# Loading the first group of x in two pieces, both ahead of the opening barrier, in a fused LoRA kernel

## The chip, the cores and the metric

One core of one Trainium2 chip. The time is device microseconds (us) of an execution, the median of several runs; of the 33 executions of the kernel before that were timed beside the experiments, 31 lie within 0.3% of the median of their call (123.17 to 123.88 us in all). The profile of an execution covers a *span*, from the first instruction to the last, which here is about 2 us less than the time (121.3 us against 123.23 us in the profiled run of the kernel before). All runs compared below are listed as fast unless the text says otherwise.

## The reference

```python
# x: (16, 512, 768), A: (768, 16), B: (16, 768), float32; scale = 0.5
def reference(x, A, B, scale):
    lora = np.matmul(np.matmul(x, A), B)
    return (x + scale * lora).astype(np.float32)
```

x is read once and the output is written once, 25.2 MB each. The arithmetic is small.

## The kernel before

The 8192 rows of x are cut into 8 groups of 1024. A group is one tile of 128 partitions with 8 rows of 768 floats each, so a partition's part of a group is 24 KB and lies in one piece in memory. Six such tiles exist. ScalarE casts a group to fp16, VectorE transposes it in blocks, TensorE multiplies by A and B, VectorE adds the product to x in place, and the tile is stored. The engines wait for each other, and for transfers, by semaphores (counters). The sync engine (SP) issues every transfer. Its first load is moved into the program's first block, ahead of the barrier at which the engines meet at the start (ScalarE's first instruction behind it comes at 0.95 us):

```python
def load(g):
    nc.sync.dma_start(out=xs[g % X_BUFS], in_=view(x2, g)).then_inc(loaded[g], 16)

def sync_program():
    ...                                   # (cut: switches symbolic addresses off and on)
    load(0)
    now, first = nc.cur_bb.bb.instructions, nc.main_func.blocks[0].instructions
    at = next(k for k, i in enumerate(first)
              if i.engine == mybir.EngineType.SP and isinstance(i, mybir.InstDrain))
    first.insert(at, now.pop())           # ahead of the barrier
    nc.sync.dma_start(out=a32..., in_=A...).then_inc(a_in, 16)   # 384 pieces of 128 B
    nc.sync.dma_start(out=b32, in_=B).then_inc(b_in, 16)         # 16 pieces of 3 KB
    for g in range(1, X_BUFS):
        load(g)
    for g in range(NG - 1):
        nc.sync.wait_ge(added, 4 * (g + 1) + 2)
        ...                               # store group g; then load groups 6 and 7

def scalar_program():
    cast(0, 0, G // 2)._wait_ge(loaded[0], 16)
    cast(0, G // 2, G // 2)
    cast(1, 0, G)._wait_ge(loaded[1], 16)
    ...                                   # (cut)
```

Of the kernel before, what the change touches and what calls it, by code (L numbers as in the profile page):

```python
# [11 lines left out]
G = 8  # L12

X_BUFS = 6
# [4 lines left out]
def kernel(  # L19
# [14 lines left out]
    nc = tc.nc  # L34
# [5 lines left out]
    x2 = x.flatten_outer_dims()  # L40
# [14 lines left out]
    xs = [x_0] + [const.tile([P, G, D], fp32, name=f"x_{i}") for i in range(1, X_BUFS)]  # L55
# [15 lines left out]
    def semaphore(name):  # L71
        sems.append(nc.alloc_semaphore(name))
        return sems[-1]

    loaded = [semaphore(f"loaded_{g}") for g in range(NG)]
# [14 lines left out]
    def view(ap, g):  # L90
        return ap[ds(g * P * G, P * G), :].rearrange("(p s) d -> p s d", s=G)

    def load(g):
        nc.sync.dma_start(out=xs[g % X_BUFS], in_=view(x2, g)).then_inc(loaded[g], 16)

    def sync_program():
        symbolic, nc._always_lower_symbolic_ap = nc._always_lower_symbolic_ap, False
        load(0)
        nc._always_lower_symbolic_ap = symbolic

        now, first = nc.cur_bb.bb.instructions, nc.main_func.blocks[0].instructions
        at = next(
            k for k, i in enumerate(first)
            if i.engine == mybir.EngineType.SP and isinstance(i, mybir.InstDrain)
        )
        first.insert(at, now.pop())
        nc.sync.dma_start(  # L107
            out=a32.rearrange("i (b r) -> i b r", b=NB),
            in_=A.rearrange("(b i q) r -> i b (q r)", i=Q, q=2),
        ).then_inc(a_in, 16)  # L110
        nc.sync.dma_start(out=b32, in_=B).then_inc(b_in, 16)  # L111
# [4 lines that stand above are left out]
            nc.sync.dma_start(out=view(out2, g), in_=xs[g % X_BUFS]).then_inc(  # L116
                freed[g] if g < len(freed) else stored, 16
            )
            if g == len(freed) - 1:
                for n in range(X_BUFS, NG):  # L120
                    nc.sync.wait_ge(freed[n - X_BUFS], 16)
                    load(n)

        nc.sync.wait_ge(added, 4 * NG + 2)
        nc.sync.sem_clear(range(nums[0], nums[-1] + 1))
# [15 lines left out]
    def cast(g, s0, n):  # L141
        rows = ds(s0, n)
        i = nc.scalar.copy(out=xh[g % 2][:, rows, :], in_=xs[g % X_BUFS][:, rows, :])  # L143
        i.then_inc(ready, 1)
        return i

    def scalar_program():
        cast(0, 0, G // 2)._wait_ge(loaded[0], 16)
        cast(0, G // 2, G // 2)
        cast(1, 0, G)._wait_ge(loaded[1], 16)  # L150
        for g in range(NG):
            for a in range(NQ):
                q = ds(a * Q, Q)
                i = nc.scalar.mul(out=y_diag[q, :, q], in_=y_ps[q, :, :], mul=sc)  # L154
                if a == 0:
                    i._wait_ge(ready, min(g + 3, NG + 1) + g + 1)
            i.then_inc(spread, 1)
            if g + 2 < NG:
                cast(g + 2, 0, G)._wait_ge(loaded[g + 2], 16)
# [86 lines left out]
    with tc.tile_critical(no_gpsimd_drain=True):  # L246
        sync_program()
        pool_program()
        scalar_program()
        vector_program()  # L250
        tensor_program()
# [37 lines left out]
```

## Time and profile before

| | before |
|---|---|
| time, median of 3 | 123.54 us (123.49 to 123.57) |
| span of the profiled run | 121.3 us |
| moved | 50.43 MB |
| first data packet, after the first issue | 1.00 us |
| mean end of the 16 DMA engines' last packets | 119.30 us |
| last engine's last packet | 120.04 us |

The last three rows are read from the DMA records of the trace, one record per packet. A packet here is one contiguous piece, 24 KB of x or of the output (2048 of the 2736 packets; the others are 384 of 128 B, 16 of 3 KB and 288 of 4 B).

The profile's page, before: busy time of the engines, then in 40 equal slices of the span the busy share of the DMA engines in tenths and the rate, then the queue's busy share. In all the profile's lines PE is TensorE and PEld its weight loads, DVE is VectorE, ACT is ScalarE, POOL is GpSimd and SPq the sync engine; L94 is line 94 of kernel.py, and x4 is a count. The page counts 16 DMA engines, and the GB/s are what they moved; what is issued to them and not yet moved is here called the queue.

```profile
PE 52.1 (43%) x323; PEld 30.6 (25%) x323; DVE 84.2 (69%) x48; ACT 55.9 (46%) x42; POOL 4.9 (4%) x9
...
DMA  7999999999999999999999999999999999999991
GB/s 227 421 392 419 397 478 413 397 478 421 397 478 405 413 470 413 413 454 430 413 446 438 413 438 446 413 438 438 421 438 438 413 446 438 413 446 438 413 454 73
...
q1 hardware_dynamic: 2736, 50.43, 97.8%
```

VectorE is the busiest compute engine, at 69%. The DMA engines are busy 97.8% of the span, and every slice but the first and the last is near full.

The stage windows, before (stretch, its length, busy time of each engine with its instructions, granted clock, DMA share, rate):

```profile
core 0: us, PE busy (x) PEld busy (x) DVE busy (x) ACT busy (x) POOL busy (x), PEclk, DMA share, GB/s
...
1.00:2.00 1.00, 0.00 (x0) 0.00 (x0) 0.00 (x0) 1.00 (x1) 0.86 (x3) 1.00 1.56 393
2.00:3.00 1.00, 0.00 (x0) 0.00 (x0) 0.00 (x0) 0.23 (x1) 1.00 (x2) 1.00 0.70 295
3.00:4.00 1.00, 0.00 (x0) 0.00 (x0) 0.00 (x0) 0.00 (x0) 1.00 (x1) 1.00 0.99 418
4.00:8.00 4.00, 0.00 (x0) 0.00 (x0) 0.00 (x0) 0.00 (x0) 1.81 (x2) 1.00 0.97 418
...
9.00:11.00 2.00, 0.00 (x0) 0.00 (x0) 0.21 (x1) 0.59 (x1) 0.00 (x0) 1.00 1.17 391
...
13.00:110.00 97.00, 50.84 (x320) 30.36 (x320) 82.10 (x44) 52.02 (x41) 0.00 (x0) 0.95 1.00 431
```

The windows book a packet whole in the stretch where it starts, so a stretch as short as a packet (0.9 us) can show over 1.00: sixteen 24 KB packets that start between 1 and 2 us make the 393 GB/s of that row, though they land later. Over long stretches this evens out: from 13 to 110 us the share is 1.00 at 431 GB/s.

The timeline, before (start, duration, engine, line, what; in brackets what the engine waited for): the first issues and the first cast, and the last two stores.

```profile
0.00 0.38 SPq L94 DMA_DIRECT2D x<-in_x_dram  x1
...
0.99 0.34 SPq L107 DMA_DIRECT2D a_70<-in_A_dram  x1
...
2.16 0.41 SPq L94 DMA_DIRECT2D x_61<-in_x_dram  x1
...
10.41 5.41 ACT L143 CAST xh_66<-x 128x3072 f16<-128x3072 f32 x2 [8.18 <-DMA x<-in_x_dram]
...
96.11 0.33 SPq L116 DMA_DIRECT2D out_dram<-x  x1
106.12 0.33 SPq L253 DMA_DIRECT2D out_dram<-x_61  x1
```

And pieces of the chain of waits that ended last, before (start, duration, what):

```profile
2.16 15.90 DMA x_61<-in_x_dram
...
18.09 5.32 ACT xh_67 L143
...
23.43 3.38 DVE xt L166
...
98.87 6.75 DVE x_61 L197 x4
```

This chain runs through ScalarE, VectorE and TensorE, and its shares by engine begin with "DVE 44%". Read alone it says that compute sets the end. The DMA records say otherwise. The last store is issued at 106.1 us, while a full group takes 8 packets of 0.912 us on each engine, 7.3 us. Work issued earlier fills the queue until about 112.7 us on the engine that ends last, so the last store is there some 6.6 us before its turn.

### The profile page before, as it was taken

The numbers are of one execution on the slowest core, as the hardware profiler recorded it, in microseconds if no ns is written. First come the engines' busy times: TensorE is split into PE (matmuls) and PEld (weight loads), VectorE is DVE, ScalarE is ACT, GpSimd is POOL, SyncE is SP. The second block draws the span as 40 slices with busy tenths as digits, with TensorE's granted clock in tenths as the row PEclk, the third lists the DMA queues.
The fourth block names the chain that finished last, engine by engine and source line by source line (L and its number), as shares of the span: only waits on it lengthen the run. The fifth ranks groups of instructions, "written<-read, shape, count | busy, mean of one in ns | idle before, by whom it ended". The sixth has DMA issues, their size and how long they took to land.

```text
span 121.3 us, 888 instructions
## 1 busy us (share of the span) xinstructions
PE 52.1 (43%) x323; PEld 30.6 (25%) x323; DVE 84.2 (69%) x48; ACT 55.9 (46%) x42; POOL 4.9 (4%) x9
## 2 busy tenths in 40 slices
PE   0003109576944684294375449437446745000000
PEld 0000006331622362172144227216213522000000
DVE  0004990299959999999999999999999639800000
ACT  4005929989159719917943395992400220000000
POOL 6900000000000000000000000000000000000000
PEclk9999999965699999999999999999999999975555
DMA  7999999999999999999999999999999999999991
GB/s 227 421 392 419 397 478 413 397 478 421 397 478 405 413 470 413 413 454 430 413 446 438 413 438 446 413 438 438 421 438 438 413 446 438 413 446 438 413 454 73
DMA packets 2736, 50.43 MB, mean 416 GB/s; under 512 B 672, under 2 KB 672, under 8 KB 688
## 3 DMA queue, kind: packets, MB, share of 16 engines
q1 hardware_dynamic: 2736, 50.43, 97.8%
HBM read 25.26 MB, written 25.17 MB: 416 GB/s over the span
## 4 chain that ended last, share of the span: by engine, by line
DVE 44%; PE 22%; DMA 13%; ACT 6%; SPq 1%; issue 1%
DVE xt L166 19%; PE y_ps L224 16%; DMA x_61<-in_x_dram 13%; DVE x_61 L197 8%; DVE x L197 5%; PE lora_ps_79 L238 5%; ACT xh_67 L143 4%; DVE x_65 L197 3%; DVE x_63 L197 3%; DVE x_64 L197 3%; DVE x_62 L197 3%; ACT y_diag L154 1%; PE lora_ps_78 L238 1%; SPq L111 1%; SPq L107 0%
## 5 line engine op out<-in xcount | busy, mean ns | idle before, releaser
L224 PE MATMUL y_ps<-xt,a_diag 128*128 128x256 f16 x192 | 24.8, 287 | 5.8 <-DVE xt L166 5.8
L238 PE MATMUL lora_ps_78<-b_rep,y_diag 128*128 128x512 f16 (+1 forms) x64 | 14.1, 346 | 27.9 <-ACT y_diag L154 14.1
L154 ACT ACTIVATE y_diag<-y_ps 32x256 f16<-32x256 f32 x32 | 12.0, 375 | 28.0 <-PE y_ps L224 27.7
L224 PEld LDWEIGHTS y_ps<-xt,a_diag 128*128 128x128 f16 x192 | 19.3, 101 | 11.6 <-DVE xt L166 6.5
L166 DVE STREAM_TRANSPOSE xt<-xh_67 128x3072 uint32<-128x3072 uint32 x4 | 13.5, 3378 | 5.9 <-ACT xh_67 L143 5.1
L238 PE MATMUL lora_ps_79<-b_rep,y_diag 128*128 128x512 f16 (+1 forms) x64 | 14.4, 351 | 6.1 <-DVE x_61 L197 1.7
L143 ACT CAST xh_66<-x 128x3072 f16<-128x3072 f32 (+1 forms) x3 | 10.7, 3604 | 10.3 <-DMA x<-in_x_dram 10.3
L166 DVE STREAM_TRANSPOSE xt<-xh_66 128x3072 uint32<-128x3072 uint32 (+1 forms) x5 | 13.6, 2728 | 1.8 <-PE y_ps L224 1.8
L238 PEld LDWEIGHTS lora_ps_78<-b_rep,y_diag 128*128 128x128 f16 x64 | 5.1, 100 | 35.8 <-issue 16.6
L143 ACT CAST xh_67<-x_61 128x6144 f16<-128x6144 f32 x2 | 10.6, 5312 | 2.3 <-DMA x_61<-in_x_dram 2.3
L238 PEld LDWEIGHTS lora_ps_79<-b_rep,y_diag 128*128 128x128 f16 x64 | 5.9, 103 | 13.2 <-DVE x_61 L197 2.4
L197 DVE TENSOR_TENSOR x_61<-x_61,lora_ps_78 128x1536 f32<-128x1536 f32 x4 | 7.0, 1741 | 2.8 <-PE lora_ps_78 L238 2.8
L175 DVE CAST a_73<-a_70 32x384 f16<-32x384 f32 x1 | 0.3, 349 | 10.8 <-DMA a_70<-in_A_dram 10.8
L197 DVE TENSOR_TENSOR x_61<-x_61,lora_ps_79 128x1536 f32<-128x1536 f32 x4 | 7.0, 1744 | 0.0
L197 DVE TENSOR_TENSOR x<-x,lora_ps_79 128x1536 f32<-128x1536 f32 x4 | 7.0, 1741 | 0.0
L197 DVE TENSOR_TENSOR x<-x,lora_ps_78 128x1536 f32<-128x1536 f32 x4 | 6.9, 1729 | 0.0
L143 ACT CAST xh_66<-x_62 128x6144 f16<-128x6144 f32 x1 | 5.3, 5313 | 0.4 <-DMA x_62<-in_x_dram 0.4
L143 ACT CAST xh_67<-x_63 128x6144 f16<-128x6144 f32 x1 | 5.3, 5314 | 0.0
L143 ACT CAST xh_67<-x_65 128x6144 f16<-128x6144 f32 x1 | 5.3, 5313 | 0.0
L143 ACT CAST xh_66<-x_64 128x6144 f16<-128x6144 f32 x1 | 5.3, 5312 | 0.0
L209 PE MATMUL lora_ps_78<-a_73,rep 32*128 32x384 f16 x1 | 0.5, 496 | 11.2 <-DVE a_73 L175 11.2
L197 DVE TENSOR_TENSOR x_62<-x_62,lora_ps_79 128x1536 f32<-128x1536 f32 x2 | 3.5, 1742 | 0.0
(23 smaller groups left out, 35.5 us busy)
## 6 DMA issues: line engine op xcount, KB each, us to landing
x<-in_x_dram SPq DMA_DIRECT2D x2, 3072.0 KB, 12.5
x_61<-in_x_dram SPq DMA_DIRECT2D x2, 3072.0 KB, 15.2
out_dram<-x SPq DMA_DIRECT2D x2, 3072.0 KB, 19.1
out_dram<-x_61 SPq DMA_DIRECT2D x2, 3072.0 KB, 15.8
x_62<-in_x_dram SPq DMA_DIRECT2D x1, 3072.0 KB, 22.7
x_63<-in_x_dram SPq DMA_DIRECT2D x1, 3072.0 KB, 29.6
x_64<-in_x_dram SPq DMA_DIRECT2D x1, 3072.0 KB, 36.3
x_65<-in_x_dram SPq DMA_DIRECT2D x1, 3072.0 KB, 43.1
```

Of the source, the lines that this page charges most:

```text
L111: nc.sync.dma_start(out=b32, in_=B).then_inc(b_in, 16)
L143: i = nc.scalar.copy(out=xh[g % 2][:, rows, :], in_=xs[g % X_BUFS][:, rows, :])
L154: i = nc.scalar.mul(out=y_diag[q, :, q], in_=y_ps[q, :, :], mul=sc)
L166: i = nc.vector.transpose(out=xt[:, rows, :].rearrange("p s w -> p (s w)"), in_=xh[g % 2][:, rows, :].rearrange("p s d -> p (s d)").bitcas ...
L175: nc.vector.tensor_copy(out=a16, in_=a32)._wait_ge(a_in, 16).then_inc(setup_dve, 1)
L197: nc.vector.tensor_tensor(out=rows, in0=rows, in1=lora_ps[n % 2], op=mybir.AluOpType.add)._wait_ge(ups, n + 1).then_inc(added, 1)
L209: nc.tensor.matmul(a_ps, rep, a16, start=True, stop=True)._wait_ge(setup_dve, 1).then_inc(setup_pe, 1)
L224: i = nc.tensor.matmul(y_ps, a_diag[:, k, :], xt_mm[:, :, k // 2, :, k % 2], start=(k == 0), stop=(k == 2 * NB - 1),)
L238: i = nc.tensor.matmul(flat[:, ds(c0, w)], y_diag[:, s + k, :], b_rep[:, ds(c0 - k * D, w)], start=True, stop=True,)
```

## The change

The load of group 0 is cut in two: row 0 of every partition (128 pieces of 3 KB), then rows 1 to 7 (128 pieces of 21 KB). Both are moved ahead of the barrier, in that order. Both count on the same semaphore, and the first cast waits for both. The intent is a quicker start of the queue: a short transfer first, with the rest close behind it.

```diff
--- before.py
+++ after.py
@@ -90,12 +90,16 @@
     def view(ap, g):
         return ap[ds(g * P * G, P * G), :].rearrange("(p s) d -> p s d", s=G)
 
-    def load(g):
-        nc.sync.dma_start(out=xs[g % X_BUFS], in_=view(x2, g)).then_inc(loaded[g], 16)
+    def load(g, s0=0, n=G):
+        rows = ds(s0, n)
+        nc.sync.dma_start(
+            out=xs[g % X_BUFS][:, rows, :], in_=view(x2, g)[:, rows, :]
+        ).then_inc(loaded[g], 16)
 
     def sync_program():
         symbolic, nc._always_lower_symbolic_ap = nc._always_lower_symbolic_ap, False
-        load(0)
+        load(0, 0, 1)
+        load(0, 1, G - 1)
         nc._always_lower_symbolic_ap = symbolic
 
         now, first = nc.cur_bb.bb.instructions, nc.main_func.blocks[0].instructions
@@ -103,7 +107,8 @@
             k for k, i in enumerate(first)
             if i.engine == mybir.EngineType.SP and isinstance(i, mybir.InstDrain)
         )
-        first.insert(at, now.pop())
+        for _ in range(2):
+            first.insert(at, now.pop())
         nc.sync.dma_start(
             out=a32.rearrange("i (b r) -> i b r", b=NB),
             in_=A.rearrange("(b i q) r -> i b (q r)", i=Q, q=2),
@@ -145,7 +150,7 @@
         return i
 
     def scalar_program():
-        cast(0, 0, G // 2)._wait_ge(loaded[0], 16)
+        cast(0, 0, G // 2)._wait_ge(loaded[0], 32)
         cast(0, G // 2, G // 2)
         cast(1, 0, G)._wait_ge(loaded[1], 16)
         for g in range(NG):
```

## The prediction

> **What bounds the kernel now.** Data movement. In the stage windows the DMA share is 1.00 at 430 GB/s from 20 to 110 us of the 121.3 us span; the DMA table gives 97.8% busy over the whole span for 50.43 MB. The busiest compute engine, VectorE, is at 69%. [...] The chain of waits runs through compute (VectorE 44%), but that is not the limit: the last store is issued at 106.1 us and lands about 14 us later, while by the DMA records one 3 MB transfer takes about 7.3 us (8 packets per engine, 0.912 us each). So the queue still held about 6.6 us of older work, and compute has about that much slack at the end.
>
> Only the edges of the queue can move. The first load is issued at 0.00 and nothing moves before 1.00 us. In the DMA records 13 engines start their first 24 KB packet at 1.00 to 1.28 us, three at 1.69 to 1.75; these packets end at 2.4 to 3.2 us, mean 2.8. At 0.912 us from 1.0 they would end at 1.9: the start-up costs about 0.9 us. The last packet ends at 120.0, the span at 121.3.
>
> **What the change does.** The same bytes move. The first load becomes 128 packets of 3 KB, then 128 of 21 KB. Cast, transpose and matmul keep their order and start no earlier: the first cast waits for both loads (count 32).
>
> Costs:
> - one more issue ahead of the barrier, 0.33 to 0.38 us like the others. A, B and the load of group 1 are issued that much later, but queue behind 7 us of group 0; GpSimd's setup ends at 5.8 us against a first use near 10.8. Off the critical path.
> - eight packets and one semaphore write more per engine. A 3 KB packet (B's) took 121 ns where 912/8 is 114; a semaphore write took 9 ns. About 0.05 to 0.1 us, on the DMA path.
>
> Gain: if part of the start-up grows with the size of the first packet [...], 3 KB packets shorten it[...]. Against it: three engines' first 24 KB packets took only 0.97 to 1.04 us, so much of the start-up seems a fixed delay. The second load is issued 0.4 us after the first, while eight 3 KB packets need about 0.9 us, so no gap opens between them.
>
> I weigh these to a net gain of about 0.2 us. Nothing later amplifies it: every later stage is the same full queue.
>
> **Prediction.** 123.3 us, 8 in 10 between 122.9 and 123.75. Faster by over 2%: 0.01; within 2%: 0.98; slower by over 2%: 0.01.
>
> **What would show it.** DMA windows: first bytes still about 1.0 us after the first issue; by 4 us up to 0.3 MB more moved than before if the size matters, the same if the start-up is fixed. Share 1.00 at 430 GB/s from 20 to 110 us. A and B issued about 0.35 us later, landing at about the same time. First cast at 10.2 to 10.5 us (10.41 before). The last store issued near 106 us, its landing moved by just what the front gained.
>
> **What would make it wrong.** 21 KB packets running below 27 GB/s per engine; engines idle near 2 us between the two first loads; the second issue delaying the start of the first; the span moving while the front does not, which would mean that the queue ran empty somewhere that I read as full.

The sum of the forecast is 123.5 us, the time of the kernel before, less a net gain of about 0.2 us: 123.3 us. That only the edges of the queue can move rests on the share of 1.00 at 430 GB/s alone. What is left is the cost, worked out from the trace of the kernel before (eight packets of 121 ns in place of 912 ns are 0.06 us more, a semaphore write 0.009 us), and the gain, which was my estimate: the 0.2 us cannot be worked out. The 0.3 MB by 4 us is my estimate too. The 27 GB/s per engine is 24 KB in the measured 0.912 us.

## The result, and the profile after

| | before | changed |
|---|---|---|
| time, median of 4 runs each, one chip | 123.52 us | 123.35 us (123.29 to 123.41) |
| ratio of the fast runs, 95% interval | | 0.9991 (0.9973 to 1.0008) |
| span of the profiled run | 121.3 us | 121.5 us |
| time of the profiled run | 123.23 us | 123.41 us |

A ratio is the mean time of one kernel's fast runs over that of the other's in the same rounds, so it is not quite the ratio of the medians that are quoted. The interval holds 1: no difference is shown. The one trace of before fell on a run of 123.23 us, below all the timed runs in this table and the one above; the trace of the changed kernel fell on its longest run. A difference of 0.1 to 0.2 us between these two traces is therefore not by itself an effect of the change.

The profile's page, changed kernel, same lines:

```profile
PE 51.1 (42%) x323; PEld 30.5 (25%) x323; DVE 84.2 (69%) x48; ACT 55.9 (46%) x42; POOL 4.9 (4%) x9
...
DMA  8999999999999999999999999999999999999991
GB/s 236 389 411 412 397 445 453 397 429 461 405 429 461 405 429 461 405 421 469 405 421 469 405 421 469 405 421 461 413 429 453 405 445 445 405 453 445 397 461 65
...
q1 hardware_dynamic: 2880, 50.43, 97.8%
```

The stage windows, changed kernel:

```profile
core 0: us, PE busy (x) PEld busy (x) DVE busy (x) ACT busy (x) POOL busy (x), PEclk, DMA share, GB/s
...
1.00:2.00 1.00, 0.00 (x0) 0.00 (x0) 0.00 (x0) 0.58 (x1) 0.39 (x2) 1.00 0.90 147
2.00:3.00 1.00, 0.00 (x0) 0.00 (x0) 0.00 (x0) 0.71 (x1) 1.00 (x3) 1.00 1.55 568
3.00:4.00 1.00, 0.00 (x0) 0.00 (x0) 0.00 (x0) 0.00 (x0) 1.00 (x1) 1.00 0.82 344
4.00:8.00 4.00, 0.00 (x0) 0.00 (x0) 0.00 (x0) 0.00 (x0) 2.28 (x2) 1.00 1.00 425
...
9.00:11.00 2.00, 0.00 (x0) 0.00 (x0) 0.15 (x1) 0.52 (x1) 0.00 (x0) 1.00 1.16 381
...
13.00:110.00 97.00, 49.86 (x320) 30.32 (x320) 82.16 (x44) 52.08 (x41) 0.00 (x0) 0.95 1.00 430
```

The row from 1 to 2 us falls from 393 to 147 GB/s and the next rises from 295 to 568. That is only the booking: 3 KB packets start all along the first two stretches, and 21 KB packets are booked where they start. To compare the starts, spread each packet's bytes evenly over its own duration and add up what has moved by a given time (worked out from the DMA records):

| MB moved by | 3 us | 8 us | 20 us | 100 us |
|---|---|---|---|---|
| before | 0.485 | 2.621 | 7.599 | 42.090 |
| changed | 0.487 | 2.577 | 7.541 | 42.040 |

At 431 GB/s, 0.1 us is 0.043 MB. The changed kernel is level at 3 us, 0.1 us behind at 8 us, and stays 0.10 to 0.13 us behind, in this one pair of traces.

The timeline, changed kernel, same lines:

```profile
0.00 0.85 SPq L95 DMA_DIRECT2D x<-in_x_dram  x2
...
1.47 0.33 SPq L112 DMA_DIRECT2D a_70<-in_A_dram  x1
...
2.65 0.42 SPq L95 DMA_DIRECT2D x_61<-in_x_dram  x1
...
10.48 5.40 ACT L148 CAST xh_66<-x 128x3072 f16<-128x3072 f32 x2 [7.77 <-DMA x<-in_x_dram]
...
96.49 0.33 SPq L121 DMA_DIRECT2D out_dram<-x  x1
106.50 0.33 SPq L258 DMA_DIRECT2D out_dram<-x_61  x1
```

The two issues ahead of the barrier take 0.85 us in place of 0.38, so A is issued 0.48 us later and group 1's load 0.49 us later. The first cast starts 0.07 us later, and the last store is issued 0.38 us later.

### The profile page after: what moved, and what is told of

The parts are those of the page before. It is cut to its first block, busy times and chain, and to the rows that moved or that the text cites. A ratio compares the mean times of both kernels' runs of the same rounds, so it can differ in the third digit from the quotient of the medians.

```text
span 121.5 us, 889 instructions
## 1 busy us (share of the span) xinstructions
PE 51.1 (42%) x323; PEld 30.5 (25%) x323; DVE 84.2 (69%) x48; ACT 55.9 (46%) x42; POOL 4.9 (4%) x9
## 2 busy tenths in 40 slices
DMA packets 2880, 50.43 MB, mean 415 GB/s; under 512 B 688, under 2 KB 688, under 8 KB 832
## 3 DMA queue, kind: packets, MB, share of 16 engines
q1 hardware_dynamic: 2880, 50.43, 97.8%
## 4 chain that ended last, share of the span: by engine, by line
DVE 44%; PE 22%; DMA 13%; ACT 6%; SPq 1%; issue 1%
DVE xt L171 19%; PE y_ps L229 16%; DMA x_61<-in_x_dram 13%; DVE x_61 L202 8%; DVE x L202 5%; PE lora_ps_79 L243 5%; ACT xh_67 L148 4%; DVE x_62 L202 3%; DVE x_65 L202 3%; DVE x_64 L202 3%; DVE x_63 L202 3%; ACT y_diag L159 1%; PE lora_ps_78 L243 1%; SPq L116 1%; SPq L112 0%
## 5 line engine op out<-in xcount | busy, mean ns | idle before, releaser
L229 PE MATMUL y_ps<-xt,a_diag 128*128 128x256 f16 x192 | 25.5, 292 | 5.9 <-DVE xt L171 5.9
L243 PE MATMUL lora_ps_78<-b_rep,y_diag 128*128 128x512 f16 (+1 forms) x64 | 13.2, 328 | 28.6 <-ACT y_diag L159 13.8
L243 PE MATMUL lora_ps_79<-b_rep,y_diag 128*128 128x512 f16 (+1 forms) x64 | 13.7, 339 | 6.7 <-DVE x_61 L202 1.7
```

The source lines that it names most:

```text
L229: i = nc.tensor.matmul(y_ps, a_diag[:, k, :], xt_mm[:, :, k // 2, :, k % 2], start=(k == 0), stop=(k == 2 * NB - 1),)
L243: i = nc.tensor.matmul(flat[:, ds(c0, w)], y_diag[:, s + k, :], b_rep[:, ds(c0 - k * D, w)], start=True, stop=True,)
```

## The account of the span

Because the steady part runs at one rate, the whole span can be laid out as a sum. For the kernel before: 1.00 us until the first packet; 50.43 MB at 0.4312 MB per us, 116.96 us; what was lost between 1 and 8 us against that rate, 0.92 us; what was lost between 8 and 13 us, 0.45 us; 0.02 us from 13 to 100. This makes 119.35 us, against a measured mean end of 119.30. One engine ends 0.74 us after the mean, at 120.04 us, and 1.25 us later the span ends. Why one engine ends later than the others is not shown; the records do not name the engines. The same account for every trace, all in us:

| kernel | lost 1 to 8 | lost 8 to 13 | last engine after the mean | span |
|---|---|---|---|---|
| before | 0.92 | 0.45 | 0.74 | 121.3 |
| changed | 1.02 | 0.47 | 0.80 | 121.5 |
| again (changed, second trace) | 1.10 | 0.54 | 0.69 | 121.5 |
| seven_first | 1.14 | 0.44 | 0.76 | 121.7 |
| rest_after_barrier | 1.22 | 0.45 | 1.08 | 121.9 |
| rest_again | 1.18 | 0.39 | 0.64 | 121.5 |
| half_after_barrier | 1.05 | 0.51 | 0.77 | 121.5 |
| eight_rows | 1.57 | 0.88 | 1.24 | 122.9 |
| hold_issues | 1.08 | 1.13 | 0.73 | 122.0 |
| hold_groups | 0.94 | 0.41 | 0.72 | 121.2 |
| early_cast | 0.95 | 0.48 | 0.79 | 121.3 |

Seven traces have the changed kernel's two loads at the front, whatever follows: changed, again, hold_issues, hold_groups, early_cast, late_2 (1.05) and late_4 (1.04). Their loss between 1 and 8 us is 0.94 to 1.10 us, mean 1.03. The one trace of before has 0.92, so a difference of 0.1 us is suggested and not shown.

## The experiments

Twelve kernels ran (two of them were repeats), all with correct results. They ran in three calls, four on a chip each; every call has its own runs of the kernel before (medians 123.48, 123.50 and 123.26 us). Edits are shown against the changed kernel unless said otherwise.

### again: the changed kernel once more

No edit.

> The changed kernel itself, unedited, to tighten the interval and to have a second trace. Theory F (fixed start-up: the first microsecond and the ramp after it do not depend on the packet size; the eight extra packets cost about 0.1 us): ratio to before 1.000 to 1.001, and the bytes moved by 8 us again about 0.04 MB below before. Rival S (the start-up shortens with a small first packet and outweighs the extra packets): ratio 0.997 to 0.999.

Measured: 123.40 us (123.11 to 123.76), ratio 0.9996 (0.9975 to 1.0017). By 8 us 2.542 MB had moved, 0.08 MB below before, where the fixed start-up let expect 0.04. This fits the fixed start-up in direction. The interval does not exclude the gain of 0.1 to 0.3% that the rival allowed; the trace speaks against it.

### seven_first: the large piece first

```diff
-        load(0, 0, 1)
-        load(0, 1, G - 1)
+        load(0, 0, G - 1)
+        load(0, G - 1, 1)
```

> The same two loads in the other order: 128 packets of 21 KB first, then 128 of 3 KB. The packets are the same in number and size, only the first one per engine is large. Theory F: the same time as the changed kernel on this chip, within 0.1 us. Rival S: slower than the changed kernel by 0.2 to 0.5 us (about 123.6 to 123.9 us), because the first packet is again large and the extra packets remain.

Measured: 123.43 us (123.19 to 123.75), ratio 0.9999 (0.9979 to 1.0019), so 0.03 us from the changed kernel's median on this chip. By 8 us 2.527 MB had moved, against 2.542 for the changed kernel beside it. Between these two traces the large piece first costs 0.015 MB, or 0.03 us. But the loss of this trace, 1.14 us, lies above those of all seven traces with the small piece first (0.94 to 1.10), so an effect of the first packet's size of about 0.1 us is not excluded; the 0.2 to 0.5 us of the rival is not seen.

This trace shows something else that its edit does not touch: the last store is issued 5.23 us later than before, at a lower mean granted clock (0.895 against 0.914), and the run took 123.57 us.

```profile
111.35 0.33 SPq L258 DMA_DIRECT2D out_dram<-x  x1
```

### rest_after_barrier: the second piece after the barrier

```diff
         load(0, 0, 1)
-        load(0, 1, G - 1)
 ...
-        for _ in range(2):
-            first.insert(at, now.pop())
+        first.insert(at, now.pop())
+        load(0, 1, G - 1)
```

> Only the one-row load is ahead of the barrier; the seven-row load is issued after it, before A. The barrier, A and B move back to about where they were before (A at about 1.4 us, barrier released at 0.95 us). Theory F: within 0.1 us of the changed kernel, because the eight 3 KB packets plus the ramp last until about 2.4 us and the second load's packets are there by about 2.0 us. Rival G (the second issue ahead of the barrier is what keeps the queue fed): 0.3 to 0.6 us slower, with engines idle near 2 us.

Measured: 124.81 us (123.78 to 125.80, the longest slow), ratio 1.0097 (1.0061 to 1.0134). The fixed-start theory, with my reading that the second load would be there in time, was wrong on this one: the kernel is about 1% slower and scatters. The rival was right in direction. In the DMA records 13 of the 16 engines pass from row 0 to the second load without a pause, and three stand idle for 1.06 us in all, most of it (at least 0.79 us) on one engine. But the changed kernel has such pauses too, and the first packets of the second load are slow besides; see half_after_barrier.

### eight_rows: eight pieces of one row

```diff
-        load(0, 0, 1)
-        load(0, 1, G - 1)
+        for s in range(G):
+            load(0, s, 1)
 ...
-        for _ in range(2):
+        for _ in range(G):
 ...
-        cast(0, 0, G // 2)._wait_ge(loaded[0], 32)
+        cast(0, 0, G // 2)._wait_ge(loaded[0], 16 * G)
```

> Group 0 in eight loads of one row, all ahead of the barrier: 64 packets of 3 KB per engine in place of 8 of 24 KB, seven more completion writes per engine, and seven more issues ahead of the barrier than before (about 3.3 us). Theory F with a cost per packet: 64 x 0.121 - 8 x 0.912 = 0.45 us, plus 7 x 0.009 = 0.06 us, so about 0.5 us above before (about 124.0 us). Rival B (an issue ahead of the barrier costs its own duration): about 3 us above before. Rival S with small packets favourable: at or below before. The first cast should still start near 10.4 to 11 us.

Measured: 124.67 us (124.05 to 125.28), ratio 1.0094 (1.0064 to 1.0124), 1.2 us above before. The issues ahead of the barrier took 3.76 us together, so the rival by which each costs its own length falls. The 0.5 us reckoned for packets is there (0.65 us more lost between 1 and 8 us than before), but so are 0.43 us more between 8 and 13 us and 0.50 us more of spread between engines; together 1.58 us, which is the difference of the spans, 1.6 us. The first cast started at 11.66 us, later than expected. Splitting further is a loss.

### hold_issues: A, B and groups 1 to 5 issued only at 6.3 us

The added wait is for the end of GpSimd's setup, which pool_done counts.

```diff
+        nc.sync.wait_ge(pool_done, 2)
         nc.sync.dma_start(out=a32..., in_=A...)
```

> The changed kernel with one more wait: the sync engine issues A, B and groups 1 to 5 only after GpSimd's setup (about 6.3 us), while group 0's two loads are moving and still some 3 us before they end. New theory H (issuing further loads while group 0 is moving slows its packets: they ran at 415 GB/s or less between 3 and 5 us, and the runs that issue more in that stretch, the one-row-ahead and the eight-row kernels, lost most): group 0's 21 KB packets run at 799 ns from the first, the bytes moved by 6 us rise by 0.05 to 0.1 MB and the time falls by 0.1 to 0.3 us. Theory F (the ramp is fixed): bytes by 6 us and time unchanged within 0.1 us.

Measured: 124.15 us (123.91 to 124.95), ratio 1.0081 (1.0052 to 1.0110). Theory H falls: holding the other issues back did not mend the start (1.08 us lost between 1 and 8 us, within the range of the other traces with this front, 0.94 to 1.10), and the rest of the loss moved to where group 1 begins. Stage windows of this kernel, to be set beside the same row of the kernels above:

```profile
9.00:11.00 2.00, 0.08 (x1) 0.09 (x1) 0.35 (x1) 0.69 (x1) 0.00 (x0) 1.00 1.08 258
11.00:13.00 2.00, 1.23 (x3) 0.14 (x3) 1.84 (x4) 2.00 (x2) 0.00 (x0) 1.00 0.94 393
```

From 9 to 11 us the rate is 258 GB/s where before had 391 and the changed kernel 381. In the DMA records the 16 packets that begin group 1 took 1.54 us on average, against 1.19 us before and 0.912 us for a plain one. They had been issued at 7.21 us and their turn came near 10.0.

### hold_groups: only groups 1 to 5 held until 6.3 us

The theory L of the expectation (a load must be issued some time ahead of its turn) is tested further under half_after_barrier.

```diff
         nc.sync.dma_start(out=b32, in_=B).then_inc(b_in, 16)
+        nc.sync.wait_ge(pool_done, 2)
         for g in range(1, X_BUFS):
             load(g)
```

> As the kernel that held A, B and groups 1 to 5 until 6.3 us, but A and B are issued at their usual time and only groups 1 to 5 wait, to about 6.3 us; the queue reaches them near 9.6 us, 3.3 us later. There the first packets of group 1 took 1.54 us on average and 0.7 us of transfer was lost between 8 and 13 us against before. Theory L: still a loss, smaller, with first packets of group 1 at 1.3 to 1.5 us, time 123.6 to 123.9 us. Rival A (issuing A with its 384 small pieces late held group 1 up): first packets as in the changed kernel (1.2 to 1.3 us) and time within 0.15 us of it.

Measured: 123.21 us (123.07 to 123.31), ratio 0.9988 (0.9972 to 1.0005). Stage windows:

```profile
9.00:11.00 2.00, 0.00 (x0) 0.00 (x0) 0.32 (x2) 0.59 (x1) 0.00 (x0) 1.00 1.21 418
11.00:13.00 2.00, 1.29 (x3) 0.23 (x3) 1.85 (x5) 2.00 (x1) 0.00 (x0) 1.00 0.95 406
```

Nothing more is lost than in the kernel before (0.41 us between 8 and 13 us, 0.45 before): group 1's first packets took 1.16 us. Group 1 was issued at 6.31 us and begun near 9.6 us. So group 1's load may be issued only 3.3 us ahead of its turn without cost. This fits rival A, that the cost in the run above came from A, with its 384 pieces, issued late. It is not shown: in the run above group 1 was also issued 0.90 us later, 2.8 us ahead of its turn, and the pair does not separate the two. This is the lowest median of all, but its interval holds 1.

### half_after_barrier: four rows before the barrier, four after

```diff
-        load(0, 0, 1)
-        load(0, 1, G - 1)
+        load(0, 0, G // 2)
 ...
-        for _ in range(2):
-            first.insert(at, now.pop())
+        first.insert(at, now.pop())
+        load(0, G // 2, G // 2)
```

> Four rows ahead of the barrier, four after it: the second load is issued at the same time as in the one-row-ahead kernel (about 1.0 us) but the queue reaches it some 2.5 us later (near 5.5 us in place of 2.2 to 3.1 us). Theory L (a load must be issued some microseconds before the queue reaches it, or its first packets stall): the second load's first packets take their plain time (about 455 ns for 12 KB) and the time is 123.4 to 123.6 us, within 0.2 us of before. Rival G2 (any issue of x between barrier and A is what costs, whenever it is reached): 124 us or more, as in the one-row-ahead kernel (1.0097 and 1.0062 of before).

Measured: 123.40 us (123.28 to 123.64), ratio 1.0006 (0.9988 to 1.0023). The second load is issued when it was in rest_after_barrier, and no cost is seen here. How the engines pass to the second load, from the DMA records (its first packet on each of the 16 engines, and the time that engines stood idle just before it, added up):

| kernel | second load issued | its turn, mean | first packets, mean | a plain one | idle, 16 engines together |
|---|---|---|---|---|---|
| changed | 0.5 us | 2.70 us | 945 ns | 799 ns | 0.45 us |
| again | 0.5 us | 2.87 us | 862 ns | 799 ns | 0.50 us |
| rest_after_barrier | 1.0 us | 2.66 us | 1098 ns | 802 ns | 1.06 us |
| rest_again | 1.0 us | 2.63 us | 1183 ns | 802 ns | 0 |
| half_after_barrier | 1.0 us | 5.69 us | 460 ns | 460 ns | 0 |

With 4.7 us between issue and turn every one of the 16 packets is plain. With some 2.3 us (seven traces with the changed kernel's front, 848 to 945 ns) they take 50 to 150 ns more on average, and with 1.6 us 300 to 380 ns more; in both some take over 1 us. So the place between barrier and A is not what costs. Theory L, that the time ahead of its turn counts, fits but is not shown: in half_after_barrier the turn itself is 3 us later, past the slow first microseconds of the queue (of the 0.92 us that the kernel before loses between 1 and 8 us, 0.87 us are lost by 3 us), and the packets are of other sizes. The first three microseconds alone may be what makes a load that comes late costly. No run gives a short lead to a load whose turn comes after the start-up, with nothing else changed.

### rest_again: rest_after_barrier a second time

No edit against rest_after_barrier.

> The kernel with only the one-row load ahead of the barrier, again, for a second time and a second trace, since the first timed runs scattered from 123.78 to 125.8 us. Theory E (one of the 16 DMA engines comes out of group 0 late and[...] ends late): the time is again 124 us or more and in the DMA records one engine's last packet ends over 1 us after the mean of the 16. Rival: the first result was chance of that chip and session: 123.4 us, the last engine 0.7 us after the mean as in the kernel before.

Measured: 123.42 and 124.99 us, ratio 1.0062 (1.0006 to 1.0118). The loss was seen again in one of the two runs, and the scatter with it; the interval of two runs only just excludes 1. The profile fell on the run of 123.42 us, in which the last engine ended 0.64 us after the mean, as before. So theory E did not show here: the 0.25 us more lost at the start is seen, but the runs of 125 us left no trace, and where their other 1.3 us went stays open.

### late_2 and late_4: compute made later on purpose

Two or four more casts of half a group ahead of the first one. Each waits for the one before by a semaphore, so there is no race, and each writes the same values, so the result is right.

```diff
+        rows = ds(0, G // 2)
+        for k in range(2):                      # 4 in late_4
+            i = nc.scalar.copy(out=xh[0][:, rows, :], in_=xs[0][:, rows, :])
+            i._wait_ge(loaded[0], 32) if k == 0 else i._wait_ge(delayed, k)
+            i.then_inc(delayed, 1)
-        cast(0, 0, G // 2)._wait_ge(loaded[0], 32)
+        cast(0, 0, G // 2)._wait_ge(delayed, 2)
```

> The changed kernel with two more casts of half a group (2.75 us each) on ScalarE ahead of the first one, so that the chain of compute starts later: the cast of group 1, on the chain of waits, moves from 18.1 to about 21.6 us, 3.4 us later. Theory F (the queue sets the end, compute has 6.6 us to spare): last store issued at about 109.5 us, time unchanged within 0.2 us. Rival C (the chain of compute sets the end, as the chain of waits draws it): 3.4 us slower, about 126.9 us.

> The same with four more casts: the cast of group 1 moves to about 27 us, 8.9 us later, past the 6.6 us to spare. Theory F: last store issued at about 115 us, the queue empty before it for about 3 us, time 2 to 4 us above the changed kernel (125.5 to 127.5 us). Rival C: about 9 us slower. Rival D (compute has far more to spare than read): unchanged.

Measured, late_2: 123.49 and 123.68 us (fast), 125.42 and 125.44 us (slow); the ratio, 1.0114 (1.0059 to 1.0169), has slow runs in it. The timeline of the run of 123.49 us:

```profile
111.85 0.33 SPq L264 DMA_DIRECT2D out_dram<-x  x1
```

The last store is issued 5.73 us later than before (111.85 against 106.12; I had expected 3.4 us, as the delay passed through group 0's own cast, transpose and matmul and not through group 1's cast) and the time is that of before. If the chain of compute set the end, this run would have taken 129 us. In it the last engine ended only 0.24 us after the mean, because most engines had caught up and waited for the last store: in the DMA records the 16 engines stood idle from about 111.8 us on, 0.6 us each on average, and the first packet of the last store starts at 112.68 us, 0.83 us after its issue. The account of the kernel before had left these 0.83 us out. There the engines come to the last store at 112.0 us on average (mean end less 7.3 us) and the last at 112.7, so the estimate is 5.1 us to spare on average and 5.8 us on the engine that ends last, in place of 6.6. seven_first fits: at a delay of 5.23 us its engines were idle for 0.1 us each. At late_2's delay nothing is left to spare, which may be why half of the runs were longer; they left no trace.

Measured, late_4: 128.96, 129.03 and 129.90 us (slow), 126.89 us (fast). The delay is 11.1 us (last store issued at 117.24 us). In the profiled run, a slow one, the queue runs dry already in the middle:

```profile
50.00:60.00 10.00, 5.79 (x40) 3.61 (x40) 9.74 (x6) 6.54 (x6) 0.00 (x0) 1.00 0.73 312
60.00:70.00 10.00, 5.79 (x40) 3.61 (x40) 9.74 (x6) 6.54 (x6) 0.00 (x0) 1.00 1.00 393
```

A share of 0.73 from 50 to 60 us is 2.7 us without transfer. In the same trace the queue is dry again before the last store, from about 116.7 us until its first packet at 118.07, 0.83 us after the issue. The span is 5.4 us longer than before for a delay of 11.1, which leaves 5.7 us that cost nothing, near the 5.8 us above. This is one run, listed as slow because it lies over 1.5% above the fastest of the four; its granted clock, 0.943, is not below that of before. The one fast run cost 3.4 us, but it left no trace, so its delay is not known.

### early_cast: row 0 used as soon as it lands

```diff
-        load(0, 0, 1)
+        load(0, 0, 1, row_in)                   # its own semaphore
 ...
-        cast(0, 0, G // 2)._wait_ge(loaded[0], 32)
+        one = nc.scalar.copy(out=xh[0][:, ds(0, 1), :], in_=xs[0][:, ds(0, 1), :])
+        one._wait_ge(row_in, 16)
+        cast(0, 1, G // 2 - 1)._wait_ge(loaded[0], 16)
```

> The changed kernel with the use that the split seems made for: row 0 has its own semaphore and ScalarE casts it as soon as it lands (about 4.5 us), and rows 1 to 3 in a second cast when the rest lands. Theory F (queue-bound, compute has over 5 us to spare): the first cast starts near 4.5 us in place of 10.5, the time is within 0.3 us of before. Rival C (chain of compute): 0.5 us or more faster.

Measured: 123.30 us (123.21 to 123.46), ratio 1.0000 (0.9978 to 1.0022). Timeline:

```profile
3.62 0.83 ACT L154 CAST xh<-x 128x768 f16<-128x768 f32 x1 [0.90 <-DMA x<-in_x_dram]
...
10.72 4.76 ACT L149 CAST xh<-x 128x2304 f16<-128x2304 f32 x2 [6.28 <-DMA x<-in_x_dram]
```

The first cast starts at 3.62 us, 7 us earlier, and the time stays. But the work behind it does not start earlier: the second cast waits for the rest of group 0, the first transpose starts at 15.07 us (14.87 before), and the last store is issued no earlier than in the changed kernel (106.50):

```profile
106.65 0.33 SPq L261 DMA_DIRECT2D out_dram<-x  x1
```

So the run shows that casting row 0 early brings nothing. What an earlier start of the whole chain would be worth, it does not test.

### ab_on_act: an attempt at a faster kernel

Against the kernel before: one load of group 0, with A and B issued from ScalarE's queue, also ahead of the barrier. The two small tiles get fixed addresses, as group 0's tile already has.

```diff
-        nc.sync.dma_start(out=a32..., in_=A...).then_inc(a_in, 16)
-        nc.sync.dma_start(out=b32, in_=B).then_inc(b_in, 16)
+        nc.scalar.dma_start(out=a32..., in_=A...).then_inc(a_in, 16)   # ahead of the barrier
+        nc.scalar.dma_start(out=b32, in_=B).then_inc(b_in, 16)         # ahead of the barrier
```

> Aimed at a faster kernel: the kernel before (one load of group 0), with A and B issued from ScalarE's queue ahead of the barrier, so that their small packets move while group 0 starts up and not between groups 0 and 1, where 0.45 us of transfer is lost in every trace. If the loss belongs to the small packets at that place and the start-up can hide them: 0.2 to 0.45 us faster than before (123.1 us), A landing near 3 us. If the small packets cost the same wherever they run: unchanged. Compute starts earlier either way, which should not matter.

Measured: 132.93 us (131.18 to 135.79, the two longest slow), ratio 1.0682 (1.0630 to 1.0735). Two views, the DMA issues (KB, us to landing) and VectorE's waits (us in all, times, longest):

```profile
a<-in_A_dram ACTq DMA_DIRECT2D x1, 48.0 KB, 25.6
b<-in_B_dram ACTq DMA_DIRECT2D x1, 48.0 KB, 26.2
```

```profile
DVE a L181 <- DMA a<-in_A_dram: 25.7, 1, 25.7
```

The half that was aimed at came true: between 8 and 13 us only 0.02 us was lost, in place of 0.45 (by the table of the account 0.39 to 0.54 us, except in eight_rows and hold_issues, where A and B are issued later). But A landed at 25.7 us and not near 3. In the DMA records A's 128-byte pieces start at the pace of one per engine and per 24 KB packet: 16 of them in most stretches of 0.912 us, from 3.4 to 23.9 us, on a queue of their own (q10 of the DMA view: 432 packets, 0.10 MB). At that pace A's 384 pieces, 24 per engine, take 22 us. Compute began some 15 us late, past what it has to spare, as in late_4 only more so.

## Why the prediction was right, point by point

The measured 123.35 us lies in the stated range and 0.05 us from the forecast. That closeness is luck: the forecast counted on a gain of 0.2 us that no run shows, and the range of 0.85 us holds a kernel without any gain as well.

- **Bound by the queue: right.** 1.00 of the DMA engines' time at 430 to 431 GB/s from 13 to 110 us in both kernels; a last store issued 5.7 us later left the time where it was (late_2's two fast runs).
- **Compute has about 6.6 us to spare: right in kind, about 1 us too large.** The 0.83 us from the issue of a store to its first packet was left out. The traces give 5.1 us on average over the engines and 5.8 us on the last; a delay of 5.23 us cost 0.1 us of idle time per engine, 5.73 us cost 0.6, and 11.1 us lengthened the span by 5.4.
- **One more issue ahead of the barrier is off the critical path: right, its length a little short.** A came 0.48 us later and not 0.35; eight issues, 3.76 us, did not cost their own length either.
- **Eight more packets and one semaphore write cost 0.05 to 0.1 us: fits, but is not shown.** The start lost 1.03 us on average over seven traces against 0.92 in the one trace of before, which fell on a quick run. Timing does not resolve this: the intervals are some 0.2 us wide on each side.
- **A gain from the small first packet that more than pays for the extra ones, net 0.2 us: not there.** This is the term that was mis-sized. The start lost no less with 3 KB packets than with 24 KB ones, and with the same two pieces in the other order the time was the same (123.43 against 123.40 us). That the start-up depends on the size of the first packet is not seen; an effect of 0.1 us, set off by the extra packets, is not excluded. My own counter-argument in the prediction was the better half of it. The median of 123.35 us lies 0.17 us below before on that chip, but the interval holds 1, the trace shows no gain, and the second measurement gives 0.08 us, so I do not read the agreement with 123.3 us as support for that term.
- **No gap opens between the two loads: not quite.** In the seven traces with this front the engines stood idle there for 0, 0, 0.02, 0.06, 0.45, 0.50 and 0.73 us, all 16 together, mostly on one engine. Averaged over the engines that is at most 0.05 us, so the time does not show it. But it was close: with the second load issued 0.5 us later, rest_after_barrier was about 1% slower.

What stays open: why the queue loses 0.9 to 1.1 us as it starts, with first packets of 3, 12, 21 and 24 KB alike; whether rest_after_barrier pays for the short lead of its second load or for a turn that falls into this start; the runs of 125 us of rest_after_barrier; and which engine ends last, since the records do not name engines.

## What to carry to other kernels

When the queue is full from end to end, lay out the span as bytes over the steady rate plus the losses at its edges, and ask of a change which term it touches. Here a start that was cut finer left the edge as it was and added packets. The chain of waits can run through compute and still not set the time (here its shares begin with DVE 44%, and a last store issued 5.7 us later left the time where it was): compare when the last store is issued with when its turn comes, and count the time from issue to first packet (0.83 us here). Look how far ahead of its turn a load is issued: in these runs 3.3 us were enough for a load of x; 1.6 us, at the start of the queue, were not. And look when small pieces land if they are put on a second queue beside large ones and something waits for them: here 48 KB took 25.6 us to land, and the kernel was 6.8% slower.
